# A streaming encoder's order of work: from a scheduler's choice to one written pipeline

## Chip, cores and metric

One core of one Trainium2 chip. The time is the device time of one execution in microseconds. Within the core, TensorE (PE) multiplies, VectorE (DVE), ScalarE (ACT) and GpSimd (POOL) do the rest, and SyncE (SP) issues most transfers. An engine works through its own queue in the order in which the program has it there.

## What is computed

Two layers over 256 positions of 1024 features, each of three sublayers: a half-step SwiGLU feed-forward (FFN), a mixer, and another half-step FFN. The mixer of layer 0 is a gated MLP (gMLP) with 128-position windows, that of layer 1 attention over chunks of 64 with a learned bias by distance. Keys and values are projected once, from the stream after layer 0. Before each sublayer the stream is scaled and shifted, behind it gated and normalised, with vectors made from c by large matrix-vector products.

```python
for l in range(DEPTH):
    mod = (c_act @ w_ada[l] + b_ada[l]).reshape(B, 1, N_MOD, D)   # shift, scl, gate, three of each
    h = x * (1.0 + scl[0]) + shift[0]
    x = layer_norm(ALPHA * x + 0.5 * gate[0] * swiglu(h, ffn_gu[l, 0], ffn_down[l, 0]), ...)
    h = x * (1.0 + scl[1]) + shift[1]
    y = gmlp_mixer(h, ...) if l < N_A else chunk_band_attention(h, w_q, rel_bias, w_o, k_pad, v_pad)
    x = layer_norm(ALPHA * x + gate[1] * y, ...)
    h = x * (1.0 + scl[2]) + shift[2]
    x = layer_norm(ALPHA * x + 0.5 * gate[2] * swiglu(h, ffn_gu[l, 1], ffn_down[l, 1]), ...)
# swiglu(h) = (silu(g) * u) @ w_down with g, u = split(h @ w_gu)
```

## The kernel before

**Products.** Each float32 operand is split into two fp32r parts, a rounded one (hi) and the rest (lo), and a product is three matmuls: xh·wh, xl·wh, xh·wl. A weight comes in units of 128 rows by 1024 columns (512 KB): SP loads raw, ACT casts hi (L190), DVE subtracts lo (L191). Positions form two halves of 128, t = 0 and t = 1. `gemm_pass` runs all units of a block over one half, six matmuls of 512 columns per unit (`mm_unit`, L234 to L238), first t = 0, then t = 1 with the same units.

**Activations.** The stream X[t] lies in fast memory by position. For a sublayer, `make_h` transposes X on PE in two groups of four (hp, L301), ACT scales and shifts each (hf, L289) and casts hh (L270), DVE subtracts hl (L271). Inside an FFN, ACT makes silu (sg, L395), DVE the product a (L396), PE transposes it (tp, L277), ACT and DVE split it again (th, tl). In the gMLP, sp is the mixing matmul over V and us its product with u.

**Sublayer end.** The last chunk of the down projection runs column half by column half (`n_outer`). Then, on DVE for each t, `add_y` multiplies by the gate (gy, L326) and adds to X (L331), and `normalise` makes the statistics (st L339, aggr L341, rs L343), a power on POOL (rs, L344), and the normalised X (L350). The hp of the next sublayer needs that X. At the end of the second FFN two modulations are made of one X, for the next FFN and for keys and values.

**Vectors from c.** 160 sums on DVE (`column`, L122), one for each 512 KB tile of `w_cols`, are drawn from a phase's list by `pump`, so much for each unit split.

**What sets the order.** Only `first_gu_part`, the first two blocks, stands in a written order. The rest goes through a scheduler that puts instructions where it expects their inputs to be ready; `after(n, fn)` puts off work until n unit ticks have passed, `get` splits a unit when first asked for, and `issue_after` ties small loads to a raw load before them. All small loads go through SP, the rel-bias loads of the attention (L694) too. Buffers: 6 raw, 11 pairs of hi and lo, 6 + 2 banks of the accumulators' memory.

## Time and profile before

| | |
|---|---|
| runs (us) | 1053.93, 1055.53, 1051.93; median 1053.93 |
| profiled run (us) | 1055.42, of which the span from first to last instruction is 1053.6 |
| TensorE clock, mean granted | 0.994 |
| PE busy | 1026.1 us, 97% of the span |
| DVE busy | 849.8 us, 81% |
| ACT busy | 506.1 us, 48% |
| POOL busy | 23.4 us, 2% |
| moved by DMA | 285.74 MB, mean 271 GB/s |

Matmuls are pipelined, and a busy PE is the union of overlapping matmuls; so idle time in front of a matmul, and the starts of neighbours, tell more than the busy share. Idle time of the other engines matters only where PE then waits. In a row of the timeline the brackets hold the idle time before an instruction and what ended it.

### The profile page before, as it was taken

To read this page: it belongs to the slowest core of one execution; us is meant where nothing else is said; L and a number is where in the kernel's file an instruction comes from. 1 tells how busy PE (TensorE), PEld (TensorE's weight loads), DVE (VectorE), ACT (ScalarE), POOL (GpSimd) and SP (SyncE) were. 2 spreads that over 40 slices of the span, in tenths; PEclk is the share of its full clock that TensorE was granted. 3 is DMA by queue.
4 is the path that set the end of the run, shared out by engine and by line. 5 is a ranking of instruction groups with operands and counts; after the bars stand their busy time and mean duration, and the time that the engine had idled before them with its cause. 6 is when DMAs were issued, how large, how long until landed. Compare 5 with 4: busy or idle time off the path is not lost.

```text
span 1053.6 us, 13538 instructions
## 1 busy us (share of the span) xinstructions
PE 1026.1 (97%) x4792; PEld 842.7 (80%) x4792; DVE 849.8 (81%) x1225; ACT 506.1 (48%) x710; POOL 23.4 (2%) x41
## 2 busy tenths in 40 slices
PE   8999999999999999999999999999999999999997
PEld 7888788787788778888887888887787788888886
DVE  6887987898999899888579986868988959555535
ACT  3553346452436464445447444453558556345520
POOL 0000000000000100000000000000000000000000
PEclk9999999999999999999999999999999999999998
DMA  9998899686798889999747997857898828645711
GB/s 345 387 345 290 322 347 350 215 282 255 272 343 313 259 292 341 355 328 339 274 160 259 320 355 245 274 201 280 271 351 284 290 97 274 235 160 191 248 61 40
DMA packets 111347, 285.74 MB, mean 271 GB/s; under 512 B 9904, under 2 KB 22832, under 8 KB 111280
## 3 DMA queue, kind: packets, MB, share of 16 engines
q1 hardware_dynamic: 110944, 284.86, 76.5%
q8 instruction: 37, 0.61, 0.2%
q14 instruction: 30, 0.25, 0.1%
q0 software_dynamic: 192, 0.02, 0.0%
q10 hardware_dynamic: 144, 0.00, 0.0%
HBM read 283.78 MB, written 1.07 MB: 270 GB/s over the span
## 4 chain that ended last, share of the span: by engine, by line
PE 53%; DVE 4%; issue 3%; DMA 3%; ACT 2%; POOL 1%; SPq 0%; POOLq 0%; ACTq 0%; DVEq 0%
PE acc L238 17%; PE acc L234 16%; PE acc L236 16%; PE tp L277 1%; DMA raw<-w_cols 1%; DMA raw<-w_q 1%; DVE lo L191 1%; ACT hf L289 1%; PE ob L749 1%; DMA raw<-w_o 1%; DVE st L339 1%; PE sc L702 1%; DVE raw L122 1%; POOL rs L344 1%; PE pT L725 0%
## 5 line engine op out<-in xcount | busy, mean ns | idle before, releaser
L190 ACT CAST hi<-raw 128x1024 fp32r<-128x1024 f32 x328 | 341.2, 1057 | 239.3 <-PE acc L236 65.1
L191 DVE TENSOR_TENSOR lo<-raw,hi 128x1024 fp32r<-128x1024 f32 x328 | 394.9, 1220 | 53.3 <-ACT hi L190 47.2
L234 PE MATMUL acc<-hi,hh 128*128 128x512 f32 x864 | 277.4, 396 | 1.6 <-ACT hh L270 0.9
L238 PE MATMUL acc<-lo,hh 128*128 128x512 f32 x864 | 272.9, 392 | 3.4 <-DVE lo L191 3.3
L236 PE MATMUL acc<-hi,hl 128*128 128x512 f32 x864 | 272.6, 391 | 0.0
L122 DVE CUSTOM_DVE_ANT_0 raw<-raw,c_row,bcol 128x1024 f32<-128x1024 f32 x160 | 203.8, 1278 | 16.0 <-DMA raw<-w_cols 15.8
L238 PEld LDWEIGHTS acc<-lo,hh 128*128 128x128 f32 x864 | 161.6, 188 | 39.1 <-DVE lo L191 5.6
L236 PEld LDWEIGHTS acc<-hi,hl 128*128 128x128 f32 x864 | 162.7, 189 | 34.5 <-DVE hl L271 0.4
L234 PEld LDWEIGHTS acc<-hi,hh 128*128 128x128 f32 x864 | 159.9, 189 | 35.1 <-ACT hi L190 2.4
L234 PE MATMUL acc<-hi,th 128*128 128x512 f32 (+1 forms) x432 | 145.7, 388 | 0.0
L236 PE MATMUL acc<-hi,tl 128*128 128x512 f32 (+1 forms) x432 | 143.7, 384 | 0.0
L238 PE MATMUL acc<-lo,th 128*128 128x512 f32 (+1 forms) x432 | 143.1, 384 | 0.1
L238 PEld LDWEIGHTS acc<-lo,th 128*128 128x128 f32 x432 | 80.9, 189 | 16.3 <-DVE lo L191 0.5
L236 PEld LDWEIGHTS acc<-hi,tl 128*128 128x128 f32 x432 | 81.2, 189 | 15.6
L234 PEld LDWEIGHTS acc<-hi,th 128*128 128x128 f32 x432 | 80.1, 189 | 14.8
L395 ACT ACTIVATE sg<-acc 128x512 f32<-128x512 f32 (+1 forms) x48 | 26.8, 562 | 93.2 <-PE acc L238 91.3
L396 DVE TENSOR_TENSOR a<-acc,sg 128x512 f32<-128x512 f32 (+1 forms) x48 | 30.7, 643 | 44.2 <-ACT sg L395 44.0
L271 DVE TENSOR_TENSOR tl<-tp,th 128x512 fp32r<-128x512 f32 (+1 forms) x56 | 36.4, 650 | 34.6 <-ACT th L270 34.5
L270 ACT CAST th<-tp 128x512 fp32r<-128x512 f32 (+1 forms) x56 | 31.0, 554 | 69.1 <-PE tp L277 68.8
L289 ACT ACTIVATE hf<-hp,B,A 128x128 f32<-128x128 f32 x96 | 36.6, 477 | 55.8 <-PE hp L301 55.8
L326 DVE TENSOR_TENSOR gy<-acc,gate 128x512 f32<-128x512 f32 (+1 forms) x49 | 32.1, 675 | 18.7 <-PE acc L238 18.6
L344 POOL TENSOR_TENSOR rs<-rs,mhalf 128x1 f32<-128x1 f32 x14 | 14.7, 1049 | 675.6 <-DVE rs L343 675.6
(101 smaller groups left out, 626.5 us busy)
## 6 DMA issues: line engine op xcount, KB each, us to landing
raw<-w_cols SPq DMA_DIRECT2D x160, 512.0 KB, 5.4
raw<-ffn_gu SPq DMA_DIRECT2D x160, 512.0 KB, 5.5
raw<-ffn_down SPq DMA_DIRECT2D x88, 512.0 KB, 5.3
raw<-w_in SPq DMA_DIRECT2D x32, 512.0 KB, 5.5
raw<-ffn_gu SPq DMA_DIRECT2D x32, 256.0 KB, 4.2
...
```

The source lines that it names most:

```text
L122: nc.vector.tensor_tensor_reduce(out=raw, in0=raw, in1=c_row, scale=1.0, scalar=bcol[:, ci, j:j + 1], op0=ALU.mult, op1=ALU.add, accum_out ...
L190: nc.scalar.copy(hi, raw)
L191: last["lo"] = eng.tensor_tensor(lo, raw, hi.bitcast(F32), op=ALU.subtract)
L234: nc.tensor.matmul(acc, lhsT=xh, rhs=wh[:, sl], start=k == 0, stop=False)
L236: nc.tensor.matmul(acc, lhsT=xl, rhs=wh[:, sl], start=False, stop=False)
L238: nc.tensor.matmul(acc, lhsT=xh, rhs=wl[:, sl], start=False, stop=k == nk - 1)
L270: nc.scalar.copy(hi, src_ps)
L271: nc.vector.tensor_tensor(lo, src_ps, hi.bitcast(F32), op=ALU.subtract)
L289: nc.scalar.activation(hf[:, sl], tp[:, sl], AF.Identity, bias=B[:, j:j + 1], scale=A[:, j:j + 1])
L326: nc.vector.tensor_tensor(tmp, acc[:, :c1 - c0], g[:, sl], op=ALU.mult)
L395: nc.scalar.activation(sg[:, :wd], g, AF.Silu)
L396: nc.vector.tensor_tensor(av[:, :wd], u, sg[:, :wd], op=ALU.mult)
```

## The change

The whole program now stands in a written order on all five engines (`manual_schedule` over SP, PE, DVE, ACT and POOL).

- All weight units form one list, `stream`. `begin` opens a block, `tick` comes after each unit (half a tick for a column half), and `prep` then splits units up to a mark that runs evenly, 6 units ahead (8 in the last chunk of a sublayer).
- The sums are one queue, `SUMS`; a rate for each sublayer gives credit by tick, up to 3. While the last chunk runs they are held (`quiet`), but for the last three units of the first column half of t = 1.
- Everything else is put off by ticks: the second half of a split (LAG_S 1, LAG_HL 2), transposes, the pieces of V's norm (LAG_V), the affine part of the residual (LAG_R), probabilities, and the k and q transposes (LAG_T).
- `add_y` and the statistics come after each column half (`last_y`).
- `mm_unit` issues xh·wh and xh·wl for a column half, then the next, then xl·wh.
- N_WARM goes from 46 to 28 transposes. The load of c goes from ACT to SP. X, lncols, b_s and w_s are loaded before the third block of the first FFN, not behind it. The gMLP's 8 bias tiles and the 12 rel-bias loads go from SP to ACT; a rel bias is loaded two groups ahead, behind the exps of a group.

The diff, cut to its core:

```diff
-LAG_A = 4
-LAG_H = (4, 4)
+LAG_A = 3
+LAG_H = 4
 LAG_H2 = 2
-LAG_M = 2
-LAG_G = 3
-LAG_R = (20, 16)
-N_WARM = (6, 46)
+LAG_R = ((12, 16), (12, 16))
+LAG_S = 1
+LAG_HL = 2
+LAG_T = 1.5
+LAG_V = ((5, 8, 28, 32), (5, 9, 30, 36))
+AHEAD = 6
+AHEAD_H = 8
+LAG_G = 8
+N_WARM = (6, 28)
...
+SUMS = [(0, 2), (0, 4), (0, 3), (0, 5), (0, 7), (0, 6), (0, 8), (1, 1), (1, 0), ("kv", 1), ("kv", 0),
+        (1, 2), (1, 4), (1, 3), (1, 5), (1, 7), (1, 6), (1, 8)]
...
-    def pump():
-        ada["credit"] += 1.0
-        while ada["steps"] and ada["credit"] >= ada["steps"][0][0]:
-            cost, s = ada["steps"].pop(0)
-            ada["credit"] -= cost
-            s()
...
+    def pump(n):
+        left, rate = ada["rate"][0]
+        ada["credit"] = min(ada["credit"] + n * rate, 3.0)
+        if len(ada["rate"]) > 1:
+            ada["rate"][0] = (left - n, rate)
+            if left - n <= 0:
+                ada["rate"].pop(0)
+    def run_sums(full):
+        if sums and ada["credit"] >= (2.0 if full else 1.0):
+            ada["credit"] -= 1.0
+            sum_step(*sums.pop(0))
...
+    def prep_hi():
+        n = now["hi"]
+        raw = load_raw(stream[n])
         hi = unitp.tile([P, D], F32R, tag="hi", name=nm("hi"))
+        nc.scalar.copy(hi, raw)
+        part_[n] = raw, hi
...
+    def prep(to, soon=0):
+        free = min(now["freed"] + N_UNIT, len(stream))
+        done_ = now["lo"]
+        while now["lo"] < min(soon if now["lo"] > done_ else max(int(to), soon), free):
+            prep_lo()
+        while now["hi"] < min(now["lo"] + 1, free):
+            prep_hi()
+        return now["lo"] > done_
+    def get(n):
+        while now["lo"] <= n:
+            prep_lo()
+        return ready[n]
+    def begin(n, ahead=AHEAD):
+        now.update(ahead=ahead, first=now["next"], n=n, ticks=NT * n, at=0.0, next=now["next"] + n)
+        return range(now["first"], now["next"])
...
                 nc.tensor.matmul(acc, lhsT=xh, rhs=wh[:, sl], start=k == 0, stop=False)
+                nc.tensor.matmul(acc, lhsT=xh, rhs=wl[:, sl], start=False, stop=False)
             for acc, sl in cols:
-                nc.tensor.matmul(acc, lhsT=xl, rhs=wh[:, sl], start=False, stop=False)
-            for acc, sl in cols:
-                nc.tensor.matmul(acc, lhsT=xh, rhs=wl[:, sl], start=False, stop=k == nk - 1)
+                nc.tensor.matmul(acc, lhsT=xl, rhs=wh[:, sl], start=False, stop=k == nk - 1)
...
-    def tick(n):
+    def tick(n, soon=0, quiet=False):
         for e in late:
             e[0] -= n
-        for e in [e for e in late if e[0] <= 0]:
+        due = [e for e in late if e[0] <= 0]
+        for e in sorted(due, key=lambda e: not e[2]):
             late.remove(e)
             e[1]()
-    def gemm_pass(xs, units, nk, nb=2, accs=None, k0=0, n_outer=False, cuts=HALVES):
+        now["at"] += n
+        full = prep(now["first"] + now["ahead"] + now["n"] * now["at"] / now["ticks"], soon)
+        pump(n)
+        if not quiet:
+            run_sums(full)
+        load_gates()
+    def gemm_pass(t, xs, units, nk, nb=2, accs=None, k0=0, cuts=HALVES, half=None):
         accs = accs or new_accs(nb)
-        for ns in ([[s] for s in range(nb)] if n_outer else [None]):
-            for ui in range(len(units)):
-                mm_unit(accs, xs, get(units, ui), ui, nk, k0, ns, cuts)
-                tick((cuts[ns[0] + 1] - cuts[ns[0]]) / D if ns else 1)
+        for ns in ([[s] for s in range(nb)] if half else [None]):
+            share = (cuts[ns[0] + 1] - cuts[ns[0]]) / D if ns else 1
+            for i, n in enumerate(units):
+                mm_unit(accs, xs, get(n), i, nk, k0, ns, cuts)
+                if t == NT - 1 and (not ns or ns[0] == nb - 1):
+                    now["freed"] = n + 1
+                tick(share, n + 3 if t == 0 else 0, half is not None and not (t == 1 and ns[0] == 0 and i > 4))
+            if half:
+                half(ns[0], accs[ns[0]])
         return accs
...
-    def end_sublayer(t, ln, nxt):
-        normalise(t)
+    def end_sublayer(t, stats, ln, nxt):
+        mu, rs = stats.rstd()
+        for x_ in pieces(X[t], HALVES):
+            nc.vector.tensor_scalar(x_, x_, mu, rs, op0=ALU.subtract, op1=ALU.mult)
         hT[t] = []
-        after(LAG_H[t], lambda: make_h(t, 0, nxt["mods"]))
+        after(LAG_H, lambda: make_h(t, 0, nxt["mods"]))
         def second():
             make_h(t, 1, nxt["mods"])
             residual_affine(t, ln)
-        after(LAG_H[t] + LAG_H2, second)
+        after(LAG_H + LAG_H2, second)
+    def last_y(t, gate, first, done, cuts=HALVES):
+        stats = Stats(len(cuts) - 1)
+        def half(n, acc):
+            add_y(t, n, acc, gate, first, cuts)
+            stats.add(X[t][:, cuts[n]:cuts[n + 1]])
+            if n == len(cuts) - 2:
+                done(t, stats)
+        return half
...
+        def load_bias():
+            if len(bias) == len(order):
+                return
+            t, hs = order[len(bias)]
+            nk = P * (t + 1)
+            bt = bcp.tile([P, len(hs), nk], F32, tag="bc", name=nm("bias"))
+            src = bass.AP(a["rel"].tensor, hs[0] * P * RELW + 2 * P - t * P,
+                          [[RELW - 1, P], [2 * P * RELW, len(hs)], [1, nk]])
+            nc.scalar.dma_start(out=bt, in_=src)
+            nc.gpsimd.memset(bt[0:CH, :, nk - CH:nk], NEG)
+            bias[t, hs] = bt
...
+            load_bias()
+            def second():
+                nc.vector.reciprocal(m[:, 3, :], m[:, 2, :])
+                for q in range(nh):
+                    nc.vector.tensor_scalar(pr[:, q, :], pr[:, q, :], m[:, 3, q:q + 1], None,
+                                            op0=ALU.mult)
+                st[(t, hs)] = pr
+            after(LAG_T, second)
...
+        later(*((i + 3, scores, 0, g0[i:i + 1]) for i in range(4)))
         v_proj(0, units)
-        for g in groups[0]:
-            probsT(0, g)
-        for g in groups[1][:4]:
-            scores(1, g)
+        for i in range(4):
+            later((i + 0.5, probsT, 0, g0[i:i + 1]), (i + 0.5, scores, 1, g1[i:i + 1]))
+        later((5, av, 0, g0[:2]), (6, av, 0, g0[2:]))
...
+    with tc.manual_schedule(engines={ET.SP, ET.PE, ET.DVE, ET.Activation, ET.Pool}):
+        done, nxt = step(0, (20, 0.5), (0, 0.32))
+        ffn(0, 0, (0, 2), done, next_affine(0, nxt, ((0, 4), (0, 3))), PARTS1, start=load_small)
+        done, nxt = step(1, (0, 0.2))
+        gmlp((0, 5), done, next_affine(1, nxt, ((0, 7), (0, 6))))
+        done, nxt = step(2, (0, 0.33))
+        ffn(0, 1, (0, 8), done, next_affine(2, nxt, ((1, 1), (1, 0)), (("kv", 1), ("kv", 0))), PARTS2)
+        done, nxt = step(3, (0, 0.24))
+        ffn(1, 0, (1, 2), done, next_affine(3, nxt, ((1, 4), (1, 3))), PARTS3)
+        done, nxt = step(4, (0, 0.3))
+        attention((1, 5), done, next_affine(4, nxt, ((1, 7), (1, 6))))
+        step(5, (0, 0.4))
+        ffn(1, 1, (1, 8), final, lambda: load_lnrow(5), PARTS2, cuts=ENDS)
```

**DVE at the end of the first sublayer.** X_106 is the stream of t = 1 and X_105 that of t = 0; gy, X, st and rs are steps of its end. Before, from the gate product of t = 1 on:

```order
L326 TENSOR_TENSOR gy_1798<-acc_1580,gate_972 128x512
L191 TENSOR_TENSOR lo_1900<-raw_1897,hi_1899 128x1024
L331 TENSOR_TENSOR X_106<-X_106,gy_1798 128x512
L326 TENSOR_TENSOR gy_1801<-acc_1581,gate_972 128x512
L271 TENSOR_TENSOR hl_1783<-hf_1777,hh_1782 128x512
L331 TENSOR_TENSOR X_106<-X_106,gy_1801 128x512
L339 BN_STATS st_1804<-X_106 128x6 x2
L191 TENSOR_TENSOR lo_1912<-raw_1909,hi_1911 128x1024
L341 BN_AGGR mv_1807<-st_1804 128x2
L191 TENSOR_TENSOR lo_1941<-raw_1938,hi_1940 128x1024
L343 TENSOR_SCALAR rs_1809<-mv_1807 128x1
L191 TENSOR_TENSOR lo_1953<-raw_1950,hi_1952 128x1024
```
After, behind the norm of t = 0, three sums and gy, X and st of the first column half of t = 1 (gy_1790):

```order
L224 TENSOR_TENSOR lo_1810<-raw_1806,hi_1808 128x1024
L224 TENSOR_TENSOR lo_1819<-raw_1815,hi_1817 128x1024
L329 TENSOR_TENSOR hl_1784<-hf_1778,hh_1783 128x512
L224 TENSOR_TENSOR lo_1842<-raw_1838,hi_1840 128x1024
L329 TENSOR_TENSOR hl_1836<-hf_1830,hh_1835 128x512
L224 TENSOR_TENSOR lo_1861<-raw_1847,hi_1849 128x1024
L389 TENSOR_TENSOR gy_1867<-acc_1615,gate_936 128x512
L394 TENSOR_TENSOR X_106<-X_106,gy_1867 128x512
L407 BN_STATS st_1740<-X_106 128x6
L412 BN_AGGR mv_1871<-st_1740 128x2
L414 TENSOR_SCALAR rs_1873<-mv_1871 128x1
L447 TENSOR_SCALAR X_106<-X_106,mv_1871,rs_1873 128x512 x2
```
The two gate products of t = 1 stood among three lo and two hl; now the second stands behind five lo and both hl.

**PE at the start of the gMLP.** hp are the transposes of X of t = 1; acc_1826 and acc_1892 are the first accumulators of the gMLP's first block. Before, behind 35 matmuls of that block:

```order
L236 MATMUL acc_1826<-hi_1911,hl_1783 128x512
L236 MATMUL acc_1827<-hi_1911,hl_1783 128x512
L238 MATMUL acc_1826<-lo_1912,hh_1782 128x512
L301 MATMUL hp_1883<-ident,X_106 128x128 x4
L238 MATMUL acc_1827<-lo_1912,hh_1782 128x512
L301 MATMUL hp_1924<-ident,X_106 128x128 x4
L234 MATMUL acc_1826<-hi_1940,hh_1782 128x512
```
After, behind 24 matmuls of it:

```order
L278 MATMUL acc_1893<-hi_1799,hh_1783 128x512
L279 MATMUL acc_1893<-lo_1801,hh_1783 128x512
L281 MATMUL acc_1892<-hi_1799,hl_1784 128x512
L281 MATMUL acc_1893<-hi_1799,hl_1784 128x512
L364 MATMUL hp_1926<-ident,X_106 128x128 x4
L278 MATMUL acc_1892<-hi_1808,hh_1835 128x512
L279 MATMUL acc_1892<-lo_1810,hh_1835 128x512
```
The first hp of t = 1 moves from the sixth unit of the block to the end of the fourth; the second, which stood one matmul behind it, now comes two units later. It is so at all five ends, with 35 to 42 matmuls before and 24 now.

**ACT in the attention.** pr are the exps of a group of heads; the bias is that of the group two further on. Before:

```order
L711 ACTIVATE pr_6849,m_6850<-pr_6849,m_6850 128x128 x4
L711 ACTIVATE pr_6873,m_6874<-pr_6873,m_6874 128x128 x4
L190 CAST hi_7051<-raw_7049 128x1024
L711 ACTIVATE pr_6897,m_6898<-pr_6897,m_6898 128x128 x4
L190 CAST hi_7345<-raw_7343 128x1024
L711 ACTIVATE pr_6921,m_6922<-pr_6921,m_6922 128x128 x4
L190 CAST hi_7354<-raw_7352 128x1024
L735 COPY vv_7064<-acc_6941 128x512
L735 COPY vv_7066<-acc_6942 128x512
L727 COPY pTs_7073<-pT_7068 128x512
```
After:

```order
L831 ACTIVATE pr_6928,m_6929<-pr_6928,m_6929 128x128 x4
L784 DMA bias_6943<-rel 128x4x128
L831 ACTIVATE pr_6953,m_6954<-pr_6953,m_6954 128x128 x4
L784 DMA bias_6968<-rel 128x4x128
L214 CAST hi_6975<-raw_6973 128x1024
L831 ACTIVATE pr_6984,m_6985<-pr_6984,m_6985 128x128 x4
L784 DMA bias_6999<-rel 128x2x256
L831 ACTIVATE pr_7017,m_7018<-pr_7017,m_7018 128x128 x4
L784 DMA bias_7032<-rel 128x2x256
L214 CAST hi_7044<-raw_7042 128x1024
```
Behind each group's exps stands a load of a bias now; four groups follow with few casts between them in both.

## Rows read from the trace of the kernel before

**Rows 1.** By stretch: us, busy PE, PEld, DVE, ACT, POOL; clock, DMA share, GB/s.

```profile
16.00:57.00 41.00, 41.00 (x180) 33.57 (x179) 36.70 (x51) 22.71 (x31) 0.00 (x0) 1.00 1.02 384
...
196.00:333.00 137.00, 132.20 (x586) 107.07 (x587) 129.10 (x188) 66.64 (x88) 4.02 (x4) 0.99 0.80 286
...
730.00:851.00 121.00, 116.13 (x635) 94.14 (x636) 103.61 (x237) 74.03 (x157) 5.04 (x13) 1.00 0.79 273
```
**Rows 2.** Waits of PE: engine, tile, line <- releaser: total us, times, longest.

```profile
PE hp L301 <- DVE X L350: 4.3, 6, 2.6
PE acc L238 <- DVE lo L191: 3.3, 3, 2.2
PE pT L725 <- ACT pTs L727: 2.5, 2, 2.2
...
PE tp L657 <- ACT k L654: 1.9, 2, 0.9
...
PE acc L234 <- ACT hh L270: 0.9, 1, 0.9
...
PE tp L277 <- DVE us L627: 0.4, 1, 0.4
```
**Rows 3.** The same view as rows 1, a stretch behind a wait of PE.

```profile
355.10:358.50 3.40, 3.40 (x12) 2.83 (x11) 3.40 (x5) 3.31 (x10) 0.00 (x0) 0.50 0.93 296
```
**Rows 4.** Timeline of PE at the gMLP's end: start, us, instruction, idle before.

```profile
351.35 0.39 PE L238 MATMUL acc<-lo,th 128*128 128x512 f32 x1
351.57 0.39 PE L234 MATMUL acc<-hi,th 128*128 128x512 f32 x1
354.52 1.47 PE L301 MATMUL hp<-ident,X 128*128 128x128 f32 x8 [2.56 <-DVE X L350]
```
**Rows 5.** Timelines of ACT and of DVE at the end of the second block.

```profile
57.31 1.09 ACT L395 ACTIVATE sg<-acc 128x512 f32<-128x512 f32 x2 [0.70 <-PE acc L450]
...
57.94 1.29 DVE L396 TENSOR_TENSOR a<-acc,sg 128x512 f32<-128x512 f32 x2
```
**Rows 6.** Timeline of DVE at the end of the second FFN.

```profile
535.21 0.69 DVE L326 TENSOR_TENSOR gy<-acc,gate 128x512 f32<-128x512 f32 x1
535.93 0.69 DVE L331 TENSOR_TENSOR X<-X,gy 128x512 f32<-128x512 f32 x1
536.54 1.28 DVE L122 CUSTOM_DVE_ANT_0 raw<-raw,c_row,bcol 128x1024 f32<-128x1024 f32 x1
...
537.75 0.69 DVE L339 BATCH_NORM_STATS2 st<-X 128x6 f32<-128x512 f32 x1
538.47 0.21 DVE L341 BATCH_NORM_AGGREGATE mv<-st 128x2 f32<-128x12 f32 x1
...
539.62 1.00 DVE L350 TENSOR_SCALAR X<-X,mv,rs 128x512 f32<-128x512 f32 x2 [0.75 <-POOL rs L344]
543.48 0.69 DVE L271 TENSOR_TENSOR hl<-hf,hh 128x512 fp32r<-128x512 f32 x1 [2.86 <-ACT hh L270]
...
556.21 3.49 DVE L191 TENSOR_TENSOR lo<-raw,hi 128x1024 fp32r<-128x1024 f32 x3
559.61 0.68 DVE L271 TENSOR_TENSOR hl<-hf,hh 128x512 fp32r<-128x512 f32 x1
560.22 1.28 DVE L122 CUSTOM_DVE_ANT_0 raw<-raw,c_row,bcol 128x1024 f32<-128x1024 f32 x1
```
**Rows 7.** Timeline of ACT at the end of the first FFN.

```profile
197.15 1.51 ACT L289 ACTIVATE hf<-hp,B,A 128x128 f32<-128x128 f32 x4 [11.30 <-PE hp L301]
198.53 1.06 ACT L190 CAST hi<-raw 128x1024 fp32r<-128x1024 f32 x1
199.47 0.64 ACT L270 CAST hh<-hf 128x512 fp32r<-128x512 f32 x1
200.00 1.06 ACT L190 CAST hi<-raw 128x1024 fp32r<-128x1024 f32 x1
```
**Rows 8.** Transfers by line: queue, count, KB each, median us to landing.

```profile
bias<-rel SPq DMA_DIRECT2D x12, 256.0 KB, 3.7
```

More of the change, by code (lines that the diff above doesn't have):

```diff
@@ L151, in load @@
             g = gatep.tile([P, D], F32, tag="gate", name=nm("gate"))
-            small_dma(g, row.partition_broadcast(P))
+            nc.sync.dma_start(out=g, in_=row.partition_broadcast(P))
             mods[key] = g
-        after(LAG_G, load)
-    ada = {"steps": [], "credit": 0.0}
-    def ada_phase(*parts):
-        for _, s in ada["steps"]:
-            s()
-        ada["steps"] = [(units / (KD * len(keys)), s) for keys, units in parts
-                        for k in keys for s in col_slice(k)]
-        ada["credit"] = 0.0
@@ L187, in split, with load_gates @@
-    def split(raw, eng):
-        hi = unitp.tile([P, D], F32R, tag="hi", name=nm("hi"))
-        lo = unitp.tile([P, D], F32R, tag="lo", name=nm("lo"))
-        nc.scalar.copy(hi, raw)
-        last["lo"] = eng.tensor_tensor(lo, raw, hi.bitcast(F32), op=ALU.subtract)
-        return hi, lo
-    def prep(srcs):
-        w = split(load_raw(srcs), nc.vector)
-        pump()
-        return w
+        gates.append((count["loads"] + LAG_G, load))
+    def load_gates(all_=False):
+        while gates and (all_ or count["loads"] >= gates[0][0]):
+            gates.pop(0)[1]()
@@ new lines, in encoder_kernel @@
+    sums = [(key, j) for key in SUMS for j in range(KD)]
+    ada = {"rate": [(0.0, 0.0)], "credit": 0.0}
+    def pump(n):
[9 more added lines that the diff above has]
+            sum_step(*sums.pop(0))
@@ new lines, in need @@
+    def need(*keys):
+        while any(k in [k_ for k_, _ in sums] for k in keys):
+            sum_step(*sums.pop(0))
+    stream = []
+    part_ = {}
+    ready = {}
+    now = {"hi": 0, "lo": 0, "freed": 0, "ahead": 0, "first": 0, "n": 1, "ticks": 1.0, "at": 0.0,
+           "next": 0}
+    def prep_hi():
+        n = now["hi"]
+        raw = load_raw(stream[n])
+        hi = unitp.tile([P, D], F32R, tag="hi", name=nm("hi"))
+        nc.scalar.copy(hi, raw)
+        part_[n] = raw, hi
+        now["hi"] += 1
@@ L483, in first_gu_part @@
         load_x(0, 1)
-        raw = gatep.tile([P, D], F32, tag="gate", name=nm("raw"))
-        for view, src in units[0][0](raw):
-            nc.sync.dma_start(out=view, in_=src)
+        raw = load_raw(units[0][0], gatep, "gate")
         for ci, m in enumerate((sc, sh)):
@@ L526, in __getitem__, with down_chunks, down @@
             return self.store[self.t][k]
-    def down(w, r0, nk, aT, gate, first, done=None, before_last=None, cuts=(HALVES, HALVES)):
+    def down_chunks(nk):
+        cut = [0, *range(nk % KD or KD, nk + 1, KD)]
+        return list(zip(cut, cut[1:]))
+    def down(nk, aT, gate, first, done=None, before_last=None, cuts=(HALVES, HALVES)):
         accs = [None] * NT
-        cut = [0, *range(nk % KD or KD, nk + 1, KD)]
-        for k0, k1 in zip(cut, cut[1:]):
-            n = k1 - k0
-            units = row_units(w, r0 + k0, n)
-            last = k0 + n == nk
+        for k0, k1 in down_chunks(nk):
+            last = k1 == nk
+            units = begin(k1 - k0, AHEAD_H if last and done else AHEAD)
             if last and before_last:
@@ L589, in v_norm @@
                 nc.vector.scalar_tensor_tensor(v, v, mu, g, op0=ALU.subtract, op1=ALU.mult)
                 nc.vector.scalar_tensor_tensor(v, v, rs, b, op0=ALU.mult, op1=ALU.add)
+            for n in range(4):
+                after(LAG_V[t][n], lambda n=n: part(n))
         for vi in range(2):
-            c0 = GH + vi * D
-            units = row_units(w_in, 0, KD, c0)
-            bts = bias_tiles(c0)
+            units = begin(KD)
+            bts = bias_tiles(GH + vi * D)
             if vi == 1:
@@ L690, in scores @@
             nh = len(hs)
[L691 to L695 removed]
+            bt = bias[t, hs]
             sc = ps.tile([P, 512], F32, tag="ps", name=nm("sc"))
@@ L785, in attention @@
-        add_y(1, accs, gate, True, HALVES)
-        done(1)
+        for i in range(2):
+            probsT(1, g1[i])
+            scores(1, g1[i + 4])
+        before_last()
+        for i in (2, 3):
+            later((i - 1, probsT, 1, g1[i:i + 1]), (i - 1, scores, 1, g1[i + 4:i + 5]))
+        later((3, av, 1, g1[:2]), (4, av, 1, g1[2:4]), (5, probsT, 1, g1[4:6]),
+              (6, av, 1, g1[4:6]), (6.5, probsT, 1, g1[6:]), (7, av, 1, g1[6:]))
+        units = begin(KD, AHEAD_H)
+        for t in range(NT):
+            gemm_pass(t, Later(oT, t), units, KD, half=last_y(t, gate, True, done))
```

414 lines of the change are left out of this document (201 added, 213 removed).

## Prediction

> **What bounds the kernel now.** I read the table by stage first: PE is busy nearly throughout, 132.20 of 137 us in the gMLP stage and 116.13 of 121 in attention [rows 1]. TensorE does a fixed list of matmuls, so only its idle time and its clock can move the result. The same rows say where DVE has little slack: it is busy 129.10 of the 137 us and 103.61 of the 121. Next the waits of PE: hp on X 4.3 us, acc on lo 3.3, pT 2.5, the k transposes 1.9, and six smaller kinds from 0.9 to 0.4, together 3.9 (hh 0.9, a 0.9, issue 0.6, hi 0.6, sp 0.5, us 0.4) [rows 2]. Two of the waits, the lo of 2.2 us after the gMLP's sp and the hp of 2.56, are each followed by 3.4 us at a granted clock of 0.50, the lower of the two levels, 1.2 GHz (the second one is shown) [rows 3]. A stretch like that gives back half of itself, 1.7 us, if it goes.
>
> The real price of a wait is read from starts: the last matmul before the long hp starts at 351.57, hp at 354.52, 2.95 us against 0.23 for two neighbours, so 2.72 lost where the row says 2.56 [rows 4]. I add 0.16 to every wait. By place: the five sublayer ends have the hp 4.3, issue 0.6, hh 0.9, a 0.9 and 0.5 of the lo, 7.2 in some 11 waits, and one slow stretch: 7.2 + 1.8 + 1.7 = 10.7. The inside of the gMLP has 2.2 of the lo, hi, sp and us, 3.7 in 5 waits, and the other slow stretch: 6.2. Attention has pT and k, 4.4 in 4 waits: 5.0. The first FFN has the rest of the lo: 0.8. All that an order can remove is 22.7 us, about 2.2%.
>
> **The change part by part.** *Matmul order within a unit, split halves, units in a stream.* Counts of matmuls, splits and sums stay. A matmul follows the one before it every 0.23 us whichever operand changes [rows 4], so xh·wl ahead of xl·wh costs nothing; it asks for lo three matmuls earlier, 0.7 us, which a lead of six units (six times six matmuls, 8.2 us) covers. Where the lead is used up the price is the 0.7.
>
> *Start.* 18 warm-up transposes less, four of which take about 0.4 us, are 1.9 us at most. That stretch, though, is DVE's and the DMA's as much as PE's: DVE 36.70 of 41 us, 384 GB/s, the most of any stage shown [rows 1]. Bounds 0 and -1.9; I take -0.7, nearer to the fed side. The load of c on SP instead of ACT stands first in its queue either way: nothing.
>
> *Third block of the first FFN.* Before, matmuls of t = 1 stand among those of t = 0 here, and PE has work while a lo is late. Now t = 0 goes through first. DVE's second pair of a starts at 57.94 and PE has left the blocks at 57.3, when ACT starts on their result [rows 5]. Now one more lo (1.13) stands ahead of that pair; behind it come two lo, a sum, a lo, two tl, a lo, a sum, two tl and the lo of the eighth unit: the pair ends near 60, and five lo (5.7), two sums (2.4) and four tl (2.4) put that lo at 70.4. PE wants it after seven units (9.5) and four groups of transposes (1.6), at 68.2: **+2.2**. Bounds: 0, if PE itself comes late, and 3.5, if the loads of X, lncols and wsT, now ahead of this block, delay a raw by a microsecond.
>
> *First FFN, rest:* the lead covers the late lo: **-0.8**.
>
> *Sublayer ends.* This decides. Let z be PE's last matmul for t = 0. DVE's durations, start to start [rows 6]: gy 0.72, X 0.61, st 0.72, aggr to X over POOL 1.15, X twice 1.00, a sum 1.21, a lo 1.13, hl 0.61. ACT's [rows 7]: four hf 1.38, hi 0.95, hh 0.53. In the new DVE order the norm of t = 0 ends at z + 4.2, three sums at 7.8, gy, X and st of the first half of t = 1 at 9.9. The hp of t = 0 stands behind 24 matmuls (5.44), ACT starts on it at 6.1, has hh at 8.0 and three hi at 8.95, 9.9 and 10.85; the second four hf, hh and two hi follow to 14.65. So DVE's three lo end at 13.3, hl at 13.9, lo 15.0, hl 15.6, lo 16.8, and only then stand gy, X, st, aggr and norm of t = 1: the first half of X is there at 16.8 + 3.2 + 0.5 = 20.5. PE reaches hp of t = 1 after 48 matmuls, two groups of transposes and four units, at z + 17.1. It waits 3.4 in all (part of it earlier, for hl). Before, hp of t = 1 stood 35 to 42 matmuls behind, not 24, so 2.5 to 4.1 us later, with X about as late: that is why it waited so little. The order leaves this the same at three ends; at the gMLP's there are two sums, and ACT sets the pace: 3.2. At the end of the second FFN two modulations are made: each group of four costs ACT two hf and two hh, DVE two hl, and the same walk gives X at 24.7: 7.6. Sum 3 x 3.4 + 3.2 + 7.6 = 21.0. For the clock I take one slow stretch, 1.7, the bounds being none and two. Ends: 21.0 + 1.7 - 10.7 = **+12.0**. Lower bound: the 9.0 that they wait now without the clock.
>
> *Inside the gMLP.* The norm of V is spread over up to 36 ticks, sp comes one tick after the gelu, and a lead of six units stands between DVE and PE: -6.2, less 0.7 for a wait at us or tp: **-5.5**. Cover: DVE's slack, 7.9 us of 137 [rows 1]. If it is gone, see the third rival.
>
> *Attention.* The k and q transposes now stand 1.5 and 2.5 ticks behind their copies, and the pT no longer in a row: -5.0. New waits: each rel-bias load is issued by ACT behind the exps of a group, two groups ahead, and takes 3.7 us to land [rows 8], POOL's memset waits for it, DVE's max behind that, and the lo behind DVE's max; groups follow each other by a tick, 1.36 us, so a load that lands 3.7 us after its issue, with an estimated 1.9 for the max and the exps before it and the memset behind it, comes 5.6 - 2.7 = 2.9 us late, once or twice, and the lead takes about half. Bounds 0 and 5, taken 2.5: **-2.5**. The gMLP's eight bias tiles moved to ACT have a whole block of 10.9 us to land in: nothing. A rule speaks to this: the Trainium skill, page "Trainium Kernel Development and Optimization", section Key Constraints, says that DMAs issued from SP, ACT and POOL run on the same 16 engines and that using several issuers saves issue time only. By it alone the move neither speeds nor slows the loads, the new wait would be 0, and the sum 2.5 us lower; it doesn't speak of an issue that stands behind other work of its engine, which is what is priced here, and no run so far shows it.
>
> *Last FFN and tail.* PE has no wait of 0.4 us in it now; gates, sums and the output keep their places: 0.
>
> Sum: -0.7 + 2.2 - 0.8 + 12.0 - 5.5 - 2.5 = **+4.7 us**. The profiled run took 1055.42 us, 1.8 more than its span; with the change it would be 1060.1. The median of the runs is 1053.93, so 1058.6.
>
> **The rivals.** *Faster: the ends wait no more than now.* Place: the norm of t = 1. Everything hangs on DVE reaching gy at z + 16.8. If DVE reaches it by about 14, since the hi are there earlier than my walk has them, hp waits under a microsecond, and the ends cost the 9.0 of now without a slow stretch: -0.7 + 2.2 - 0.8 - 1.7 - 5.5 - 2.5 = -9.0, so 1045; without the third block's and attention's waits 1040. It decides from gy's start below z + 14. For it: before, DVE idled 2.86 us in this very stretch of the second FFN [rows 6]. Against: the order now fills that place with sums, in front of gy.
>
> *No change: the new waits are only those of the ends.* No slow clock behind them and no idle in attention: 4.7 - 1.7 - 2.5 = +0.5, 1054.4. For it: lead enough. Against: DVE's load in attention.
>
> *Slower still: DVE runs out inside the gMLP.* In order, each idle moment of DVE is lost, and it has 5.8% left there. If its waits for ACT and PE pass that 7.9 us, the lead is eaten and the 5.5 of gain goes: +10.2, 1064.1. Against: idle time of DVE overlaps the ends' waits, in which it catches up.
>
> **How the numbers follow.** Forecast 0.38 (1056 to 1061), faster rival 0.30 (1040 to 1049), no change 0.22, slower still 0.10. A measurement of this kernel tells 0.3%, 3.2 us, from nothing. Faster is the first rival: 0.30; slower the forecast's upper part and the third rival: 0.42; same the second and the forecast's lower edge: 0.28. The range takes in the faster rival's lower end and the slower one's: 1040 to 1064. The likeliest case's own is 1056 to 1061.
>
> **What would show it.** At each end the last matmul of t = 1 to the hp of t = 1: 24 matmuls and 3.4 us idle, 7.6 in the second FFN, DVE with lo and sums up to gy. Half clock behind one or two of them. No lo wait after sp. About 2 us idle in the third block. If the hp waits sum to under 10 us, the walk is wrong, and with it the sign; if PE waits for lo in the gMLP, the third rival is right.

## The result, and the profile after

The kernel got slower. Medians: 1077.76 us (1076.58 to 1079.18) against 1054.73 for the kernel before beside it, a ratio of 1.023 with a 95% interval of 1.0212 to 1.0248. The prediction was 1058.6, a range of 1040 to 1064: the sign of the forecast held, the size did not, and the time lies above the range. The profiled execution took 1077.01 us.

The page's first lines of the changed kernel, span and busy time by engine:

```profile
span 1075.2 us, 13494 instructions
PE 1035.3 (96%) x4774; PEld 847.3 (79%) x4774; DVE 858.3 (80%) x1224; ACT 503.9 (47%) x710; POOL 18.9 (2%) x41
```
PE's last matmul starts at 1066.7 us instead of 1045.6: of the 21.6 us between the two profiled spans, 21.1 stand on PE. Its waits, to be held against [rows 2]:

```profile
PE hp L364 <- DVE X L447: 15.0, 5, 5.3
PE acc L281 <- DVE hl L329: 5.9, 4, 2.5
PE tp L340 <- DVE tl L329: 3.8, 1, 3.8
PE acc L279 <- DVE lo L224: 3.5, 2, 2.8
...
PE warm L492 <- POOL ident masks.py:199: 1.4, 1, 1.4
```
The waits of pT and k (transposes of the probabilities and of k) are gone, lo is what it was, hp has grown from 4.3 to 15.0, and hl and tl are new. A wait is not the whole loss, so I also took the trace by starts: the distance from each matmul to the next, less 0.227 us for 512 columns and in proportion for narrower ones, is lost time, be it a wait, a half clock or a small gap. In us, by place (an end reaches from 6 us before its first hp to 6 us behind its last):

| place | before | after | change | predicted |
|---|---|---|---|---|
| start and first FFN | 15.0 | 18.6 | +3.6, less 1.0 for 18 transposes that are gone: +2.6 | +0.7 |
| five sublayer ends | 16.6 | 34.1 | +17.5 | +12.0 |
| inside the gMLP | 12.9 | 11.1 | -1.8 | -5.5 |
| inside attention | 15.3 | 19.2 | +3.9 | -2.5 |
| other three FFNs | 9.5 | 8.4 | -1.1 | 0 |
| sum | 69.3 | 91.4 | +21.1 | +4.7 |

**The ends.** DVE's timeline at the end of the first FFN (start, us, instruction, idle before it), the place that the prediction walked through:

```profile
193.01 0.69 DVE L389 TENSOR_TENSOR gy<-acc,gate 128x512 f32<-128x512 f32 x1 [0.74 <-PE acc L281]
...
197.27 1.28 DVE L141 CUSTOM_DVE_ANT_0 raw<-raw,c_row,bcol 128x1024 f32<-128x1024 f32 x1
...
200.89 0.69 DVE L389 TENSOR_TENSOR gy<-acc,gate 128x512 f32<-128x512 f32 x1
...
202.95 3.48 DVE L224 TENSOR_TENSOR lo<-raw,hi 128x1024 fp32r<-128x1024 f32 x3
206.34 0.68 DVE L329 TENSOR_TENSOR hl<-hf,hh 128x512 fp32r<-128x512 f32 x1
...
209.85 0.68 DVE L389 TENSOR_TENSOR gy<-acc,gate 128x512 f32<-128x512 f32 x1
...
213.11 1.00 DVE L447 TENSOR_SCALAR X<-X,mv,rs 128x512 f32<-128x512 f32 x2 [0.69 <-POOL rs L415]
```
With z at 192.9, the sums start at z + 4.3, the gy of the first half of t = 1 at 7.9, the three lo at 10.0, hl at 13.4, the last gy at 16.9 and X at 20.2. The prediction had 4.2, 7.8, 9.9, 13.3, 16.8 and 20 (X there at 20.5): the walk was right to 0.2 us. PE's timeline where that X is awaited, at this end and at three later ones, as one line of [rows 4]:

```profile
213.71 0.66 PE L364 MATMUL hp<-ident,X 128*128 128x128 f32 x4 [1.78 <-DVE X L447]
...
366.63 0.66 PE L364 MATMUL hp<-ident,X 128*128 128x128 f32 x4 [2.69 <-DVE X L447]
...
563.32 1.11 PE L364 MATMUL hp<-ident,X 128*128 128x128 f32 x4 [5.32 <-DVE X L447]
...
756.49 0.78 PE L364 MATMUL hp<-ident,X 128*128 128x128 f32 x4 [3.47 <-DVE X L447]
```
**The clock.** Stretches of PE at half clock (granted 0.50, the lower of the two levels, 1.2 GHz) in the same table by stretch as [rows 3] (us, busy PE, PEld, DVE, ACT, POOL; clock, DMA share, GB/s). Before there were two of 3.4 us; now six times 3.4:

```profile
67.40:70.80 3.40, 3.40 (x13) 2.84 (x12) 3.40 (x6) 2.47 (x4) 0.00 (x0) 0.50 1.00 375
265.40:268.80 3.40, 3.30 (x8) 2.63 (x9) 3.30 (x5) 1.02 (x1) 0.00 (x0) 0.50 0.88 280
367.80:371.20 3.40, 3.40 (x9) 2.67 (x8) 3.40 (x8) 1.65 (x4) 0.00 (x0) 0.50 0.39 115
562.30:569.10 6.80, 5.78 (x16) 4.72 (x17) 4.66 (x9) 4.15 (x10) 0.97 (x2) 0.50 0.47 145
756.90:760.30 3.40, 3.40 (x11) 2.72 (x9) 3.21 (x6) 2.12 (x5) 0.30 (x1) 0.50 0.58 195
```
The last three begin within 1.2 us of the end of the hp waits of 2.69, 5.32 and 3.47 us, the second of them a microsecond ahead of it; at the waits of 1.78 and, at the fifth end, 1.76 there is none.

**Attention.** The two kernels between the same events (6 us behind the last hp of one end, to 6 us before the first of the next), first before, then after, 511 and 512 matmul records:

```profile
753.50:846.30 92.80, 89.42 (x511) 72.52 (x509) 82.48 (x207) 57.45 (x128) 3.06 (x11) 1.00 0.84 295
```
```profile
767.70:864.20 96.50, 96.50 (x512) 75.73 (x511) 72.13 (x185) 57.85 (x127) 2.36 (x10) 1.00 0.74 245
```
PE is now busy all of the time, at full clock, and takes 3.7 us longer for the same list. The long waits did go (4.0 us of lost time in gaps over 0.25 us, now none), but the small gaps grew from 11.2 to 19.2. By the pairs of neighbours between which they stand: a score (sc) behind a score went from 2.1 to 5.2 us in all, an acc behind an acc from 0.7 to 3.0, an ob (probabilities times values) behind an ob from 1.5 to 2.7, an acc behind a score from 0.5 to 1.9 (11 such places after 3), and an acc behind an ob from none to 0.9. The timelines of PE show where, scores of t = 0 and what follows them, before and after:

```profile
788.84 2.27 PE L702 MATMUL sc<-kT,qT 64*128 64x128 f32 x26
791.04 0.72 PE L234 MATMUL acc<-hi,hh 128*128 128x512 f32 x2
```
```profile
805.08 1.16 PE L822 MATMUL sc<-kT,qT 64*128 64x128 f32 x8
806.16 0.50 PE L278 MATMUL acc<-hi,hh 128*128 128x512 f32 x1
806.50 0.39 PE L279 MATMUL acc<-lo,hh 128*128 128x512 f32 x1
```
26 scores in a row took 2.20 us, 0.085 each; 8 between two units take 1.08, 0.135 each, and the first acc behind them has its neighbour after 0.34 instead of 0.23 us. Before, 18 of the 57 scores that follow a score start within 30 ns of it; after, none of 52.

**The third block** stands with e4.

### The profile page after: what moved, and what is told of

Read it like the earlier page. It is cut to its first block, busy times and chain, and to the rows that moved or that the text cites. A ratio compares the mean times of both kernels' runs of the same rounds, so it can differ in the third digit from the quotient of the medians.

```text
span 1075.2 us, 13494 instructions
## 1 busy us (share of the span) xinstructions
PE 1035.3 (96%) x4774; PEld 847.3 (79%) x4774; DVE 858.3 (80%) x1224; ACT 503.9 (47%) x710; POOL 18.9 (2%) x41
## 4 chain that ended last, share of the span: by engine, by line
PE 79%; DVE 9%; DMA 5%; ACT 3%; issue 3%; POOL 1%; POOLq 0%; SPq 0%; DVEq 0%; ACTq 0%
PE acc L278 24%; PE acc L279 24%; PE acc L281 24%; DVE lo L224 3%; PE tp L340 2%; DVE raw L141 2%; DMA raw<-w_cols 2%; DMA raw<-ffn_gu 1%; PE sc L822 1%; ACT hi L214 1%; DMA bin<-b_in 1%; DVE st L407 1%; PE ob L874 1%; ACT hf L352 1%; DVE gy L389 1%
## 5 line engine op out<-in xcount | busy, mean ns | idle before, releaser
L214 ACT CAST hi<-raw 128x1024 fp32r<-128x1024 f32 x328 | 335.1, 1050 | 158.9 <-DMA raw<-ffn_gu 58.8
L278 PE MATMUL acc<-hi,hh 128*128 128x512 f32 x864 | 346.5, 401 | 0.0
L279 PE MATMUL acc<-lo,hh 128*128 128x512 f32 x864 | 340.6, 394 | 3.6 <-DVE lo L224 3.5
L279 PEld LDWEIGHTS acc<-lo,hh 128*128 128x128 f32 x864 | 164.4, 190 | 37.1 <-DVE lo L224 4.8
L278 PEld LDWEIGHTS acc<-hi,hh 128*128 128x128 f32 x864 | 164.4, 190 | 34.6 <-issue 1.7
L278 PE MATMUL acc<-hi,th 128*128 128x512 f32 (+1 forms) x432 | 167.2, 388 | 0.0
L279 PE MATMUL acc<-lo,th 128*128 128x512 f32 (+1 forms) x432 | 164.2, 382 | 0.0
L389 DVE TENSOR_TENSOR gy<-acc,gate 128x512 f32<-128x512 f32 (+1 forms) x49 | 33.1, 675 | 21.6 <-PE acc L281 21.5
L340 PE MATMUL tp<-ident,a 128*128 128x128 f32 x176 | 27.4, 277 | 3.8 <-DVE tl L329 3.8
```

Of the source, the lines that this page charges most:

```text
L214: nc.scalar.copy(hi, raw)
L278: nc.tensor.matmul(acc, lhsT=xh, rhs=wh[:, sl], start=k == 0, stop=False)
L279: nc.tensor.matmul(acc, lhsT=xh, rhs=wl[:, sl], start=False, stop=False)
L340: nc.tensor.transpose(tp[:, q * P:(q + 1) * P], src[:, q * P:(q + 1) * P], ident)
L389: nc.vector.tensor_tensor(tmp, acc[:, :w], mods[gate][:, sl], op=ALU.mult)
```

## The experiments

Ratios are to the kernel before, with 95% intervals. Each kernel is the changed one with the edit shown.

**e1_hp_later: the transposes of h asked for later.**

```
-LAG_H = 4
+LAG_H = (4, 6)
-        after(LAG_H, lambda: make_h(t, 0, nxt["mods"]))
+        after(LAG_H[t], lambda: make_h(t, 0, nxt["mods"]))
```


> One number: the hp of t = 1 is put off by 6 ticks behind its norm, not 4 (its second group by 8, not 6), so PE asks for X 12 matmuls, 2.7 us, later at each of the five ends. Position theory (PE asks too early for an X that comes at a fixed time): the hl waits at the ends stay (6.6 us in all), the hp waits fall from 15.8 to about 4, most of it in the second FFN; three of the six slow-clock stretches of 3.4 us go, 1.7 us each. Time 1077.8 - 12 - 5 = about 1061. Rival (DVE is the bound through the whole stretch, so what PE does not wait for at hp it waits for at lo or hl a little later): the hp waits fall but new lo or hl waits of the same size come in the next block, and the time stays above 1072.

1073.75 us, 1.0171 (1.013 to 1.0212). Waits of PE in it:

```profile
PE acc L281 <- DVE hl L329: 11.5, 7, 2.5
PE tp L340 <- DVE tl L329: 4.8, 1, 4.8
PE acc L279 <- DVE lo L224: 4.4, 1, 4.4
...
PE hp L364 <- DVE X L447: 2.0, 2, 1.3
```
hp fell from 15.0 to 2.0; 5.6 us more of hl and 4.9 more of a, tl, lo and k came in its place, and the time fell by 4.0 us, not 17. The rival was right in the main: what is late is the chain that makes X, more than hp's place in PE's order.

**e2_no_sums: no vector sums ahead of the gy of t = 1.**

```
-  tick(share, ..., half is not None and not (t == 1 and ns[0] == 0 and i > 4))
+  tick(share, ..., half is not None)
```


> The three sums (two at the gMLP's end) that stand on DVE between the norm of t = 0 and the gate product of t = 1 are taken out of that place; they come after the end instead, so the count of sums is the same. Walk of the prediction: the lo that follow wait for ACT's hi (8.95, 9.9, 10.85 behind the end of t = 0), so X of t = 1 comes only 0.2 us earlier and the ends keep 21 to 22 us of waits: 1076 to 1078. Rival (the sums are what delays X): X comes 2.4 to 3.6 us earlier at each end, the ends lose some 13 us of waits and three slow-clock stretches, 1060.

1080.54 us, 1.0224 (1.0181 to 1.0267), over the 1076 to 1078 expected, with hp 15.1 and hl 4.0: nothing won. The sums don't set the ends; without them DVE stands before the same lo and hl, which wait for ACT (at the first end 1.48 and 0.80 us for hi).

**e3_hold_split: no unit split while the second column half of t = 1 runs.**

```
-        full = prep(...)
+        full = hold or prep(...)
+                     hold: half is not None and t == 1 and ns[0] == nb - 1
```


> No unit is split (no hi, no lo) while PE runs the second column half of t = 1 in a sublayer's last chunk; the splits follow the norm. The sums stay where they are. Queue theory (the five lo between are what X of t = 1 waits for): gy starts when its matmuls end, X is there 15.5 us behind t = 0 instead of 20.5, hp never waits, and PE waits instead at the fourth unit of the next block for a lo that now comes behind the norm: about 1.4 us at four ends, 3.8 in the second FFN, 9 in all instead of 22, and two or three slow-clock stretches less: 1060 to 1062. Rival (hp would be late in any case, since X hangs on POOL and the sums): hp waits over 10 us in all, time above 1070.

1072.39 us, 1.0162 (1.0125 to 1.02). Waits of PE:

```profile
PE acc L279 <- DVE lo L224: 15.7, 10, 4.2
...
PE tp L341 <- DVE a L476: 4.0, 4, 1.3
```
The hp and hl waits are gone entirely, so the split halves ahead of the last gy were their cause. But the stream then has only three units ready behind the end, and lo is waited for at the fourth: 1.4 to 1.6 us at four ends, 4.4 at the second FFN's, 10.3 in all, about as expected. The time still missed the 1060 to 1062 expected: behind the ends the lead stays short (4.0 us for a), the gMLP's lo waits grew from 3.5 to 5.3 us, and the third block's wait for tl stayed (4.7).

**e7_one_split: the same, but one unit may be split.**

```
+                     hold: half is not None and t == 1 and ns[0] == nb - 1 and i > 0
```


> As the run that holds splitting, but one unit is still split at the start of the second column half of t = 1. Walk: gy of t = 1 at 12.2 behind the end of t = 0, the fourth unit's lo ready in time, the fifth's at 17.5 just when PE wants it: waits at hp and at those lo under 0.5 us at four ends, 3.4 in the second FFN (there 4.4 with all splits held). Sum of the ends 5 us, against 22 after and 9.5 with all held; time 1077.8 - 17 - 5 (three slow stretches) = 1056 if DVE has the slack to pay back. Rival (DVE is behind for longer than the end itself; what PE gains it loses in the next block at lo, a and tl): under half of it, 1068 to 1073, with new waits of 1 us and more on a or lo in the 40 us behind each end.

1063.51 us, 1.0054 (1.0029 to 1.0078), 14.3 us off the changed kernel with one condition. Waits of PE, and DVE's two gy at the first FFN's end:

```profile
PE acc L279 <- DVE lo L224: 6.1, 5, 2.7
...
PE hp L365 <- DVE X L448: 1.9, 1, 1.9
```
```profile
194.37 0.69 DVE L390 TENSOR_TENSOR gy<-acc,gate 128x512 f32<-128x512 f32 x1 [0.99 <-PE acc L281]
...
205.43 1.29 DVE L330 TENSOR_TENSOR hl<-hf,hh 128x512 fp32r<-128x512 f32 x2
206.64 0.68 DVE L390 TENSOR_TENSOR gy<-acc,gate 128x512 f32<-128x512 f32 x1
```
One lo and two hl stand ahead of the last gy now, not five lo and two hl. It starts 12.3 us behind that of t = 0, not 16.8. The first rival's point of decision, gy's start below z + 14, is met, and hp waits 1.9 once in the whole kernel. Lost time at the ends: 34.1 to 13.7 us. The time stayed over the 1056 expected since places elsewhere grew: first FFN 1.4, gMLP 2.6, second FFN 2.8. One half-clock stretch is left at the ends, but three more stand elsewhere (at 11.4, 66 and 264 us), so there are six as in the changed kernel.

**e9_short_sums: the vector sums over a quarter of their columns.**

```
+            w_ = slice(0, 256)      # of 1024 columns
```


> All sums behind the first two blocks take 256 of their 1024 columns (so the modulation vectors are not those of the reference): some 0.9 us less of DVE for each of 144, about 125 us of DVE work taken away; loads, order and everything else stay. Walk of the prediction (the ends wait for ACT's hi and for the lo queued ahead of gy, not for DVE's load): the ends keep 18 to 21 us of hl and hp waits, with only the lo waits of the gMLP (3.9) and their slow stretch gone, 1069 to 1073. Rival (DVE's load sets the ends): their waits fall below 8 us and the time to 1050.

1074.83 us, 1.0176 (1.0142 to 1.021), a little over the 1069 to 1073 expected. DVE is busy 111.5 us less than in the changed kernel (858.3), and the ends keep their waits, 19.2 us after 20.9:

```profile
PE 1033.1 (97%) x4774; PEld 845.7 (79%) x4774; DVE 746.8 (70%) x1224; ACT 502.9 (47%) x710; POOL 18.2 (2%) x41
```
```profile
PE hp L365 <- DVE X L448: 15.1, 5, 3.7
PE acc L282 <- DVE hl L330: 4.1, 4, 2.5
```
Together with e7: what counts at an end is what stands ahead of gy in DVE's order, and what that waits for, not how much DVE has to do.

**e6_fill: transposes of the identity ahead of the hp of t = 1,** 16 of them, 48 at the second FFN's end.

```
+FILL = {1: 16, 2: 48}
+        if t == 1 and half == 0:
+            for i in range(FILL[len(mods_)]):
+                nc.tensor.transpose(tp[:, i % 4 * P:(i % 4 + 1) * P], ident, ident)
```


> 16 transposes of the identity (48 in the second FFN) stand in front of the first hp of t = 1 at each sublayer's end and write the same tile, which the hp then overwrite: PE works for 1.7 us (5.2) of the time in which it waits for X; nothing else changes. Clock theory (a slow-clock stretch follows an idle PE, and each one costs 1.7 us by itself): the waits for X shrink by what is filled in, the total of idle and filled time stays at 22 us, and the four slow stretches behind the ends (367, two at 562, 756 us) go: 1077.8 - 4 x 1.7 = 1071. Rival (the slow stretches cost nothing of their own, since DVE is behind there anyway and PE would wait for it): time within 2 us of 1077.8.

1072.46 us, 1.0165 (1.0144 to 1.0186), 5.3 us less though PE has more to do:

```profile
PE hp L368 <- DVE X L451: 2.6, 2, 1.7
```
All four half-clock stretches behind ends are gone. By the distances of starts, with the filled transposes counted as work, the ends take 5.8 us less for it, where four at 1.7 would be 6.8 (part of the stretch at 562.3 lay in the wait itself). A stretch more stood at the start (11.4 us) and one more in the third block, which cost 1.3 us of it. This is the one run that prices the clock apart from the waits.

**e4_x_later: the loads of X, lncols and wsT behind the third block's.**

```
+   start() called behind gu_part(part[2:], aT)
```


> The loads of X, lncols, b_s and w_s are issued behind the third block of the first FFN instead of ahead of it, as in the kernel before; all else as after. DMA theory (these loads push the block's raw units back by some 3 us, so that tl is late and the transposes at 67 us wait 3.8 us, with a slow-clock stretch behind): the wait falls to under 1 us and the stretch goes, -4 to -5.5 us, 1072 to 1074. Rival (DVE's queue of lo, sums and tl is too long there, as the prediction had it): 2 us of wait remain, and the time stays within 2 us of 1077.8.

1073.5 us, 1.0167 (1.0133 to 1.0202). In the changed kernel the third block's chain begins with a raw that lands late; rows of ACT, DVE and PE:

```profile
61.32 1.05 ACT L214 CAST hi<-raw 128x1024 fp32r<-128x1024 f32 x1 [3.51 <-DMA raw<-ffn_gu]
...
62.40 1.23 DVE L224 TENSOR_TENSOR lo<-raw,hi 128x1024 fp32r<-128x1024 f32 x1 [2.03 <-ACT hi L214]
...
67.12 1.76 PE L340 MATMUL tp<-ident,a 128*128 128x128 f32 x8 [3.85 <-DVE tl L329]
```
With the loads later, this wait is 1.2 and the half clock at 67.4 is gone; the section from the 188th to the 284th full-width matmul takes 25.69 us, after 29.73 in the changed kernel and 24.22 before. So 4.0 of the 5.5 us are those loads, the half clock with them; the 1.5 left is near the 2.2 that the prediction had for DVE's queue, though PE stands before tl there, not before the lo that its walk named.

**e5_bias_sp: the gMLP's bias tiles and the rel-bias loads back on SP.**

```
-   nc.scalar.dma_start(...)     # load_bias, bias_tiles
+   nc.sync.dma_start(...)
```


> The gMLP's 8 bias tiles and the 12 rel-bias loads are issued by SP, as in the kernel before, at the same places of the program; all else as after. The prediction priced their move to ACT at 2.5 us of the attention. Theory (DVE's 6.7 us of waits for the bias in the attention come from the issue behind the exps, but PE has no long wait there, so they cost nothing): time within 2.5 us of 1077.8. Rival (the move to ACT costs what was priced, or more, since the tiles of the gMLP also land late): 1073 to 1075, with DVE's bias waits under 2 us.

1102.61 us, 1.0464 (1.0438 to 1.049): 25 us slower, against both theories. What SP's queue waits for:

```profile
SPq L784 <- DVE m L826: 49.9, 10, 12.6
...
SPq L666 <- DVE V L702: 19.6, 4, 10.6
```
Each of these loads waits for its buffer, and on SP the raw loads of the stream stand behind it: PE waits for lo 8.0 and for pT 7.8 us, and the half-clock stretches add up to 51.2 us, 15 times 3.4, where the changed kernel has 20.5. At these places of the program the move to ACT is what the written order needs, not a cost of it; SP with the loads at other places was not tried. The Trainium skill, page "Trainium Kernel Development and Optimization", section Key Constraints, says that several issuers save issue time only; here the trace differs, since an issue that waits for a buffer holds its queue.

**e8_gmlp_sums: the sums of the gMLP's modulation spread differently.**

```
-        done, nxt = step(1, (0, 0.2))
+        done, nxt = step(1, (32, 0.0), (0, 0.33))
```


> The sums of the gMLP (rate 0.2 per tick) are held for its first 32 ticks and run at 0.33 in the rest: five sums, 6 us of DVE, leave the input half, and come in its second half. Theory (DVE has no slack in the gMLP's first half: 6 us of work too many make PE wait 3.9 us for lo at 241 and 262 us and bring a slow stretch): both waits go, -3.9 -1.7, 1072. Rival (the late lo come from raw units that arrive late behind the bias and norm rows of the gMLP): the waits stay over 2.5 us, time over 1076.

1074.72 us, 1.0177 (1.0157 to 1.0197), 3.0 us less. The lo waits at 241 and 262 us are gone with the half clock behind the latter, while the ends have one half-clock stretch more, so that the time stayed over the 1072 expected. Waits of PE in it, then the changed kernel from 204 to 254 us and over the stage of [rows 1]:

```profile
PE acc L279 <- DVE lo L224: 1.1, 2, 0.7
```
```profile
204.00:254.00 50.00, 46.11 (x204) 36.95 (x203) 45.07 (x63) 25.86 (x37) 2.02 (x2) 1.00 0.84 283
196.00:333.00 137.00, 130.27 (x583) 106.43 (x582) 127.02 (x176) 65.21 (x85) 4.43 (x5) 0.99 0.81 273
```
Inside the gMLP the lost time falls from 11.1 to 6.8 us, 6.1 under the kernel before, about the gain that the prediction had. DVE idles 4.9 of the 50 us ahead of the late lo, in waits of 1.4 us and less for ACT, a load and POOL, with work standing behind. That is the third rival's mechanism, in a part of the gMLP.

**e10_three, e11_five, e12_best: the edits together.** e10 is e7, e4 and e8. e11 is e7 and e4 with

```
+        done, nxt = step(1, (24, 0.0), (0, 0.28))
+LAG_K = 2.5          # k transposes, LAG_T before
+        lag = LAG_H + (t == 1 and len(nxt["mods"]) == 2)
```
and e12 is e11 with

```
+LAG_A = 4
+            after((5, 2)[t], ...)   # the second modulation of an end
+        ffn(..., PARTS1, start=load_x)   # X behind block three, small tables a part later
```


> Three edits together: one split only in the second column half of t = 1 (alone -14.3 us), the loads of X and small tables behind the third block (alone -4.3), the gMLP's sums held for its first 32 ticks (alone -3.0). Theory (three separate causes, each at its own place): the gains add, 1077.8 - 14.3 - 4.3 - 3.0 = 1056, within 0.3% of the kernel before; the waits at 63 us and the lo waits at 237 to 265 us are gone and hp keeps under 3. Rival (all three are one shortage of DVE time that moves on): 1062 or more, with new waits for lo in the gMLP's second half.

1056.73 us, 1.0015 (0.9999 to 1.0031): within the noise the three gains add up, as expected.

> As the run with three edits, and: the k and q transposes one tick later (2.5 and 3.5 behind their block), the hp of t = 1 one tick later where two modulations are made, and the gMLP's sums held for 24 ticks and then at 0.28 per tick. The waits left are k transposes 2.3, hp 1.9, lo in the gMLP: theory 3 to 5 us less than with three edits, 1051 to 1053, at or a little under the kernel before (1055). Rival (ACT and DVE only pass the wait on to the scores or the next lo): the same as with three edits within 1.5 us.

1053.59 us, 0.9991 (0.9976 to 1.0006): 3.1 us under e10, just over the 1051 to 1053 expected, and the two intervals overlap. The longest wait left is a lo wait of 3.4 at the second FFN's end with the half clock behind it.

> As the run with five edits, and three more, each at a wait that is left there: at the end of the second FFN the second modulation (for keys and values, needed only in the attention) is put off by 5 ticks for t = 0 and 2 for t = 1, so that ACT and DVE have one modulation ahead of gy (wait for lo 3.4 with a slow-clock stretch 1.7: goes); products a are transposed 4 ticks later, as in the kernel before, not 3 (waits of tp on a, 2.8 in all: go); the loads of X come behind the third block and those of the small tables one part later (wait for lo at 102 us, 1.9: goes). Theory: 1053.6 - 5 - 2.8 - 1.9 = 1044, 1% under the kernel before. Rival (DVE is so full that each wait only moves): 1051 or more.

1050.55 us, 0.9958 (0.9942 to 0.9974): faster than both kernels, by 0.4%, 4.4 us, than before. It missed the 1044 and lies by the rival's 1051. Its page and waits of PE:

```profile
span 1049.5 us, 13493 instructions
PE 1028.6 (98%) x4774; PEld 842.3 (80%) x4774; DVE 854.1 (81%) x1224; ACT 507.9 (48%) x710; POOL 19.0 (2%) x41
```
```profile
PE acc L282 <- DVE lo L227: 3.3, 7, 0.8
PE tp L344 <- DVE tl L333: 2.5, 1, 2.5
```
By the table's count it loses 8.8 us at the ends (16.6 before) and 7.0 in the gMLP (12.9), but 20.2 in attention (15.3) and 18.4 in the start and first FFN (15.0). Of the three gains that were to come on top of e11, the second FFN's end came, 6.7 us there to 3.4. The waits for a fell from 1.9 to 0.4 us and the lo wait at 104 us went, but those for tl grew from 1.8 to 3.5, and two half-clock stretches stand in the first FFN, at 11.0 and 69.1 us, which e11 did not have: by the count neither place won. Attention's small gaps are the largest loss left, but e11 has them too.

## Why the prediction was wrong, point by point

- *Start, -0.7:* right. The first two blocks went from 56.20 to 55.20 us.
- *Third block, +2.2:* the named cost was there (1.5 left in e4), and so was the bound's other cause, loads ahead of the raw: but these were given 1.3 us and a place in the bounds, where e4 shows 4.0 with the half clock. The term by itself was off by a slip too: 57.3, 9.5 and 1.6 make 68.4, not 68.2. The rest of the FFN gained 1.9 by the table, after 0.8 predicted, which hides a part of it: 1.9 us missed in all.
- *Ends, +12.0:* the step that was to decide was right: waits 21.0 predicted, 20.9 in the rows of hp and hl, with 0.16 for each of nine 22.3. By end, 3.4, 3.2, 7.6, 3.4 and 3.4 were predicted; 3.5, 3.5, 8.2, 3.6 and 3.5 came. The mis-sized term is the clock: "one slow stretch, 1.7, the bounds being none and two". Four came, 6.8 us at 1.7 each, and e6 shows that they go with the idle time and were worth 5.8. The rows had a stretch behind 2.56 us of idle [rows 3, 4]; my own walk had five ends with more than 3 us, one with 7.6, and still counted one stretch.
- *Inside the gMLP, -5.5:* wrong, -1.8. Waits at sp went, lo waits of DVE's making came (2.8 at the longest, with its half clock). The cover that I named, DVE's slack of 7.9 us of the stage, is still there, 10.0 of 137 us now, but 4.9 of it is idle time ahead of the late lo: in a fixed order slack is no cover by itself. e8 shows that the place of the sums is the cause: with them later the gain was 6.1.
- *Attention, -2.5:* wrong in sign, +3.9, the largest miss: 6.4. The long waits went, as said (4.0). The new wait for the bias cost PE nothing: transfers on ACT's queue land in 4.1 us after 3.7 [rows 8], DVE waits 6.7 us for them in all, and PE never. What failed is the sum itself, which has waits of attention alone: scores and ob products that the new order puts between units stand in it at nothing, without a reason, and the small gaps grew by 7.9 us. The 0.23 us from matmul to matmul [rows 4] was read from neighbours of one shape. That the gaps grew most among the scores (3.2 us) and among and next to the acc, the starts show; no run changed this order by itself, and why scores no longer start in pairs stays open.
- *Move of the bias loads:* listed as a cost of 2.5 in attention, nothing in the gMLP. e5 has the opposite: without it, the places of the loads kept, the changed kernel loses another 25 us.
- *Last FFN, 0:* right, 3.2 to 3.3 us of lost time.

The misses: 1.9 + 5.5 + 3.7 + 6.4, less 1.1 for the other FFNs, is 16.4, all of the 21.1 but the 4.7 forecast. Of the rivals, the first described e7's kernel and not this one. The third was right in place and mechanism, for 3.7 of its 5.5 us; its 1064.1 had neither the ends' clock nor attention's gaps. The range fell short at the top because the ends' clock was bounded at two stretches, the third block's and the gMLP's at none, and attention had no upper end above 0. The sign was not luck: it came from the ends, whose walk held.
